# Neighbourhood attention: dividing the softmax on POOL ahead of the transposes

## The chip, the cores and the metric

One core of a Trainium2 chip. The core has five engines, each with its own queue of instructions that it takes in order: TensorE (PE: matrix products and transposes, weight loads shown as PEld), VectorE (DVE), ScalarE (ACT), GpSimd (POOL) and SyncE (SP, which here only issues DMAs). Engines wait for each other by semaphores. The metric is the device time of one execution in microseconds (us), as the median of several; smaller is better.

## What is computed

A two-layer backbone over 2048 latent tokens and 256 context tokens, 1024 wide. The first layer mixes windowed and latent attention; the second, which the change touches, is neighbourhood attention with 16 heads of 64, on a grid of 32 rows by 64 columns:

```python
def row_block(args):                       # one grid row of queries
    ...
    s_loc = einsum('bqhd,bkhd->bhqk', qr, kr) * scale + bias      # 8 x 64 keys around the row
    s_loc = where(mask, s_loc, -inf)                              # 16 columns of them
    s_ctx = einsum('bqhd,blhd->bhql', qr, kc) * scale             # all 256 context keys
    p = softmax(concatenate([s_loc, s_ctx], axis=-1), axis=-1)
    return einsum(p_loc, vr) + einsum(p_ctx, vc)
...
y = (o * silu(z)) @ out_w
h = h + gate * y;  output = rms_norm(h, final_g)
```

The softmax divides each row of exponentials by its sum. It can be divided before the product with V or after it; the change moves this division.

## The kernel before

The program runs its stages one after the other: in0 (input projection of layer 0), attn_a, attn_b, outp(0), in1 (input projection of layer 1), attn_c (the neighbourhood attention) and outp(1) (output projection, residual, last norm). Everything is float32; a product in full precision is made of passes over a rounded part ("h", type fp32r) and a remainder ("l"). Tile's scheduler sets the order of instructions on each engine from its own estimate of times; the code only proposes an order. On the chip that order is fixed.

**attn_c** (from line 1375) has 64 units: 16 heads by 4 column blocks cb of 512 queries. In a unit, `s_pieces` does four row groups rg of 128 queries: four score matmuls into PSUM (`cs`, lines 1475 to 1478, two buffers of two banks), one DVE instruction (line 1482) that adds the bias `cbias` and writes the scores to SBUF (`cp`, 128x640 or 128x768) with their row extremum `cnm`, and one ACT instruction (line 1487) that exponentiates `cp` in place and leaves the row sum in a column of `den`. `t_pieces` and `pv_pieces` (line 647 on) then turn the exponentials around for the product with V: 22 transposes of 128x128 on PE, in six blocks, block j into the PSUM tile `ptc_j` (tag `pt`, three buffers for all of them). Each block is copied out as `phc_j` by ACT (line 239) and as the remainder `plc_j` by DVE (line 240), and PE multiplies V with both into `co` (line 656). ACT copies `co` out as `cos`, and SP stores that to the scratch tensor `s_o`. The transposes of a unit are proposed two units after its scores (`queue`), and the `cp` tiles are two rings of four buffers, two units' worth. POOL makes the bias tiles `cbias` (line 1453) for three of four units.

In the names of instructions, `cp_23` is the tile of column block 2, row group 3, and `ptc_2_0`, `phc_2_0`, `plc_2_0` belong to column block 2, block 0.

Before the change `den` collects the row sums of a head. When the head is done, `den_done` calls `den_piece` (line 672 on): reciprocal on DVE, one transpose on PE (`dnc`, line 677), a copy on DVE and a store to the scratch tensor `s_rd`, 19 times in all.

**outp(1)** goes through four chunks c of 512 tokens. For each it makes G, the gated attention output, in 8 steps j: `load(j)` issues the loads of `o` (two halves), `z` and two row broadcasts of `rd` on SP's queue (lines 1133, 1134, 1136); `comp(j)` adds the halves (line 1147), multiplies by `rd` (line 1148) and by `z` (line 1149), and splits into the high part on ACT (line 1151) and the low one on POOL (line 1152). Lines 1147 and 1148 run on POOL for chunk 0, whose steps lie in attn_c's time, and on DVE for the others. Then 48 matmuls (line 1186) make each of 16 tiles of 128 tokens, with SP loading the residual `rx` (8 DMAs each, line 1172) and storing the result to `out_dram` (line 1221).

Of the kernel before, what the change touches and what calls it, by code (L numbers as in the profile page):

```python
# [8 lines left out]
F32 = mybir.dt.float32  # L9
R32 = mybir.dt.float32r  # L10
BF16 = mybir.dt.bfloat16
AF = mybir.ActivationFunctionType
ALU = mybir.AluOpType
# [3 lines left out]
P = 128  # L17
D = 1024
KB = D // P
TL = 2048  # L20
# [3 lines left out]
NTL = TL // P  # L24
# [76 lines left out]
class Kern:  # L101
    def __init__(self, ctx, tc, ins, out):
        self.tc, self.nc = tc, tc.nc
        self.i, self.out = ins, out
        nc = self.nc
        self.scr = {}

        def scr(name, shape):
            self.scr[name] = nc.dram_tensor("s_" + name, shape, F32, kind="Internal").ap()


        scr("krT", (2, 32, T))
        scr("kaT", (2, 128, T))
        scr("qaT", (2, 512, T))
        scr("qnT", (2, 512, T))
        scr("qrT", (2, 256, T))
        scr("kbT", (2, 512, T))
        scr("qcT", (2, 1024, TL))
        scr("kcT", (2, 1024, T))
        scr("va", (T, 2, 128))  # L120
        scr("vb", (T, 8, 128))

        scr("vc", (16, GRID_W, 4, 8, 128))
        scr("vx", (16, TC, 128))
        scr("z0", (1024, T))
        scr("z1", (1024, TL))
        scr("o0", (2, 1024, T))
        scr("o1", (2, 1024, TL))
        scr("rd0", (16, T))
        scr("rd1", (16, TL))  # L130
        scr("h1", (T, D))
        scr("gate", (2, 2, D))
        scr("one", (1, T))

        cp = self.pool(ctx, "const", 1)
        self.cp = cp
        self.ident = cp.tile([P, P], F32, name="ident")
        make_identity(nc, self.ident)
        self.mhalf = cp.tile([P, 1], F32, name="mhalf")
        nc.gpsimd.memset(self.mhalf, -0.5)  # L140
        one = cp.tile([P, NT], F32, name="one")
        nc.gpsimd.memset(one, 1.0)
        oner = cp.tile([P, NT], R32, name="oner")
        nc.gpsimd.tensor_copy(oner, one)
        self.oner = oner

        self.fac = [cp.tile([P, KB, 2], F32, name=f"fac{l}") for l in range(2)]
        self.sh = [cp.tile([P, KB, 2], F32, name=f"sh{l}") for l in range(2)]
        self.adab = cp.tile([P, 2, 24], F32, name="adab")
        self.ng = cp.tile([P, 2, KB], F32, name="ng")  # L150
# [927 lines left out]
    def outp(self, l):  # L1078
        nc, tc, i, scr = self.nc, self.tc, self.i, self.scr
        with ExitStack() as ctx:  # L1080
# [18 lines left out]
                fg = p.tile([P, D], F32, bufs=1, name="fg")  # L1099
                nc.sync.dma_start(fg, i["fg"].partition_broadcast(P))  # L1100
            chunks = CHUNKS[: 5 - l]
            o_, z_, rd_ = scr[f"o{l}"], scr[f"z{l}"], scr[f"rd{l}"]
            G = {}

            eslots = [(self.E, x) for x in ("vw" if l else "v")]
# [5 lines left out]
            def gsteps(c):  # L1111
                t0, n = chunks[c]
                pl = self.E if c % 2 == 0 else gp
                tags = [("qh", "ql"), ("kh", "kl")] if c % 2 == 0 else [("g0", "g1"), ("g2", "g3")]
                G[c] = [[pl.tile([P, T], R32, tag=t, name=f"G{t}{l}{c}")[:, : 4 * 512].rearrange("p (k t) -> p k t", t=512)
                         if c % 2 == 0 else pl.tile([P, 4, 512], R32, tag=t, name=f"G{t}{l}{c}") for t in tt] for tt in tags]
                ld = {}

                def load(j):
                    if c == 0 or l:  # L1120
                        if c == 0:
                            sl, tag = eslots[j % len(eslots)]
                        else:
                            sl, tag = slots[nld[0] % len(slots)]
                            nld[0] += 1
                        t = sl.tile([P, T if l == 0 else 4 * 512], F32, tag=tag, bufs=1, name=f"o{l}{c}{j}")
                        t = t[:, : 4 * 512].rearrange("p (k t) -> p k t", t=512)
                        o, z, rd = t[:, 0:2], t[:, 2:3], t[:, 3:4]
                    else:
                        o, z, rd = [lp.tile([P, m, 512], F32, tag=x, bufs=b, name=f"{x}{l}{c}{j}")  # L1130
                                    for x, m, b in (("oo", 2, 3), ("oz", 1, 2), ("ord", 1, 2))]
                    js = slice(j * P, (j + 1) * P)
                    nc.sync.dma_start(o[:, :, :n], o_[:, js, t0 : t0 + n].rearrange("e p t -> p e t"))
                    nc.sync.dma_start(z[:, 0, :n], z_[js, t0 : t0 + n])
                    for e in range(2):
                        nc.sync.dma_start(rd[e * 64 : e * 64 + 64, 0, :n],
                                          rd_[2 * j + e : 2 * j + e + 1, t0 : t0 + n].broadcast_to([64, n]))
                    ld[j] = (o, z, rd)

                def comp(j):  # L1140
                    a = ahead[c > 0]
                    if j + a < KB:
                        load(j + a)
                    o, z, rd = ld[j]
                    a = o[:, 0, :n]
                    e1 = nc.gpsimd if c == 0 and l else nc.vector
                    e1.tensor_add(a, a, o[:, 1, :n])
                    e1.tensor_mul(a, a, rd[:, 0, :n])
                    nc.vector.tensor_mul(a, a, z[:, 0, :n])
                    h, lo = [x[:, j % 4, :n] for x in (G[c][0][j // 4], G[c][1][j // 4])]  # L1150
                    nc.scalar.activation(h, a, AF.Copy)
                    nc.gpsimd.tensor_sub(lo, a, f(h))
                return [lambda j=j: load(j) for j in range(ahead[c > 0])] + [lambda j=j: comp(j) for j in range(KB)]


# [219 lines left out]
    def attn_c(self):  # L1375
# [5 lines left out]
        with ExitStack() as ctx:  # L1381
# [9 lines left out]
            pt = self.pool(ctx, "act", 3, psum=True)  # L1391
            op = self.pool(ctx, "aco", 1, psum=True)
            sp = self.pool(ctx, "acs", 2, psum=True)
            DEN = {}

            def den_of(h, cb):

                key, c0 = (h, 0) if h < 15 else ((h, cb), cb * 4)
                if key not in DEN:
                    DEN[key] = r1.tile([P, NTL], F32, tag="den", bufs=3, name=f"denc{h}_{cb}")  # L1400
                return DEN[key], c0

            def den_done(h, cb):
                if h < 15 and cb < 3:
                    return
                d, c0 = den_of(h, cb)
                n = NTL if h < 15 else 4
                self.den_piece(p, pt, d, n, scr["rd1"][h, c0 * P : (c0 + n) * P], f"c{h}_{cb}")

            rm = r1.tile([P, 3, 512], F32, bufs=1, name="rm")  # L1410
            nc.sync.dma_start(rm, i["crm"])

# [44 lines left out]
            def s_pieces(h, cb):  # L1457
# [7 lines left out]
                def go(rg):  # L1465
                    r0, nr = RG[rg]
                    nl = nr * 32
                    qs = slice(cb * 512 + rg * P, cb * 512 + rg * P + P)
                    ps = sp.tile([P, 1024], F32, tag="s", name=f"cs{h}_{cb}{rg}")
                    pl, px, al = ps[:, 512 - nl : 512], ps[:, 512:768], ps[:, 512 - nl : 768]  # L1470
                    bi = b[:, RT[rg], 512 - nl : 768]
                    pl = pl.rearrange("p (t x) -> p t x", x=P)
                    cs = slice(CS[cb] * 4, CS[cb] * 4 + P)
                    rts = slice(r0 // 4, (r0 + nr) // 4)
                    nc.tensor.matmul(pl, q[:, qs], k1v[:, rts, cs], start=True, stop=False)
                    nc.tensor.matmul(pl, q[:, qs], k2v[:, rts, cs], start=False, stop=True)
                    nc.tensor.matmul(px, q[:, qs], k1[:, TL:T], start=True, stop=False)
                    nc.tensor.matmul(px, q[:, qs], k2[:, TL:T], start=False, stop=True)  # L1478
                    n = nl + 256
                    s = pr[n].tile([P, n], F32, name=f"cp{h}_{cb}{rg}")  # L1480
                    nm = r1.tile([P, 1], F32, tag="nm", bufs=16, name=f"cnm{h}_{cb}{rg}")
                    nc.vector.tensor_tensor_reduce(  # L1482
                        out=s[:, :n], in0=al, in1=bi, scale=-1.0, scalar=3.0e38,
                        op0=ALU.add, op1=ALU.min, accum_out=nm)
                    d, c0 = den_of(h, cb)
                    col = cb * 4 + rg - c0
                    self.acts = nc.scalar.activation(s[:, :n], s[:, :n], AF.Exp, bias=nm, scale=-1.0,  # L1487
                                                     accum_out=d[:, col : col + 1]).ins
                    Pt[rg] = s
                return [lambda rg=rg: go(rg) for rg in range(4)], Pt  # L1490

# [40 lines left out]
            def emit_t(sl):  # L1532
                u = queue.pop(0)
                tl = t_pieces(*u)
                old, pend[:] = pend[:], []
                merge(sl, tl)
                den_done(u[0], u[1])
                for s in old:
                    s()

# [144 lines left out]
```

## Time and profile before

| | us |
|---|---|
| median of 3 runs (lowest to highest) | 3622.36 (3619.59 to 3623.66) |
| the profiled execution, its own time | 3611.3 |
| its span, first to last instruction | 3609.5 |
| PE busy, of the span | 3450.7 (96%) |
| DVE busy | 2302.3 (64%) |
| ACT busy | 1904.8 (53%) |
| POOL busy | 1765.0 (49%) |
| attn_c in the trace (first score matmul to the last `ptc`) | 2866 to 3401 |
| outp(1) after it, to the last instruction | 3401 to 3609.5 |

Busy shares are means over stages with different limits, and PE's busy time includes modelled ends of its matmuls. What bounds a stage is read from that stage's windows and its timeline. Times of instructions below come from the one profiled execution, 11 us shorter than the median of the runs.

### The profile page before, as it was taken

The page shows a single profiled execution, that of the slowest core. Times are in us where ns is not written, and L with a number is a line of the kernel's source. Part 1 is how long each engine was busy: PE and PEld are TensorE (multiplying, and loading weights), DVE is VectorE, ACT ScalarE, POOL GpSimd, SP SyncE. Part 2 cuts the span into 40 slices and gives each one's busy share as a digit, 9 for nine tenths or more (in the row PEclk, how much of TensorE's full clock was granted, in tenths as well). Part 3 has the DMA queues.
Part 4 walks back from the last instruction along what each step waited for, and adds up shares of the span by engine and source line. Part 5 has one row for each costly group of instructions (what it writes and reads, how often), then busy time and mean ns, then how long its engine had stood idle before and what let it go on. Part 6 is the DMA issues. An engine that isn't in the chain of part 4 may idle for free.

```text
span 3609.5 us, 52993 instructions
## 1 busy us (share of the span) xinstructions
PE 3450.7 (96%) x17607; PEld 2853.3 (79%) x17607; DVE 2302.3 (64%) x4313; ACT 1904.8 (53%) x3808; POOL 1765.0 (49%) x1655
## 2 busy tenths in 40 slices
PE   6999989999999999999989999999999999999888
PEld 5777779889877777777758778888888899999766
DVE  6445552389999999999978862203110288888565
ACT  4344333389777777777751142223222388888511
POOL 6555544211389999999982262224113133333532
PEclk8999999999999999999999999999999999999999
DMA  6758564673302332213149864544345567666685
GB/s 219 225 196 262 176 188 129 204 204 83 89 16 64 70 69 69 43 38 72 52 140 327 276 193 163 166 112 148 130 129 154 182 250 260 239 228 217 202 236 169
DMA packets 381051, 576.76 MB, mean 160 GB/s; under 512 B 35393, under 2 KB 218081, under 8 KB 370913
## 3 DMA queue, kind: packets, MB, share of 16 engines
q1 hardware_dynamic: 380777, 573.39, 52.2%
q8 instruction: 138, 2.26, 0.3%
q14 instruction: 136, 1.11, 0.1%
HBM read 399.36 MB, written 173.90 MB: 159 GB/s over the span
## 4 chain that ended last, share of the span: by engine, by line
PE 67%; DMA 14%; DVE 6%; issue 5%; POOL 4%; ACT 3%; SPq 1%; DVEq 0%; POOLq 0%; ACTq 0%
PE mm L269 7%; PE mm L268 7%; PE mm L267 7%; PE co L656 4%; DMA adat<-in_adat_dram 4%; PE bo L1000 3%; PE ptc L647 3%; PE bm L943 3%; PE bs L979 3%; PE bs L980 3%; PE bo L1001 3%; PE bs L981 3%; DMA o<-s_o 2%; PE ao L656 2%; PE pta L647 2%
## 5 line engine op out<-in xcount | busy, mean ns | idle before, releaser
L261 POOL TENSOR_TENSOR wl<-ws,wh 128x512 fp32r<-128x512 f32 (+2 forms) x320 | 425.4, 1344 | 638.1 <-ACT wh L260 571.8
L990 POOL TENSOR_TENSOR bacc<-bacc,bph 128x512 f32<-128x512 f32 (+1 forms) x528 | 668.1, 1267 | 35.3 <-ACT bph L984 2.6
L984 ACT ACTIVATE bph<-bs 128x512 fp32r<-128x512 f32 (+1 forms) x610 | 353.4, 579 | 215.0 <-PE bs L981 184.7
L945 DVE TENSOR_REDUCE bmx<-bm 128x1 f32<-128x512 f32 (+1 forms) x656 | 406.4, 628 | 58.8 <-PE bm L943 42.4
L986 DVE TENSOR_TENSOR bpl<-bs,bph 128x512 fp32r<-128x512 f32 (+1 forms) x610 | 401.0, 659 | 16.3 <-ACT bs L985 15.2
L985 ACT ACTIVATE bs<-bs 128x512 f32<-128x512 f32 (+1 forms) x610 | 350.7, 575 | 0.0
L260 ACT ACTIVATE wh<-ws 128x512 fp32r<-128x512 f32 (+2 forms) x328 | 197.5, 613 | 267.1 <-DMA ws<-in_w_dram 215.4
L1453 POOL TENSOR_TENSOR cbias<-cbu,rm 128x384 f32<-128x384 f32 x144 | 158.1, 1110 | 343.7 <-DVE cnm L1482 205.9
L267 PE MATMUL mm<-Uh,wh 128*128 128x512 f32 (+1 forms) x832 | 324.2, 390 | 0.3 <-ACT wh L260 0.3
L268 PE MATMUL mm<-Ul,wh 128*128 128x512 f32 (+1 forms) x832 | 323.7, 389 | 0.0
L269 PE MATMUL mm<-Uh,wl 128*128 128x512 f32 (+1 forms) x832 | 321.8, 390 | 0.4 <-POOL wl L261 0.4
L1482 DVE CUSTOM_DVE_ANT_0 cp<-cs,cbias 128x640 f32<-128x640 f32 (+1 forms) x256 | 222.7, 886 | 134.2 <-PE cs L1478 91.7
L1000 PE MATMUL bo<-bph,bv 128*128 128x512 f32 (+1 forms) x610 | 240.2, 394 | 15.8 <-ACT bos L1005 15.8
L979 PE MATMUL bs<-bqh,bkh 97*128 97x512 f32 (+1 forms) x610 | 242.7, 398 | 12.2 <-DVE bpl L986 11.6
L240 DVE TENSOR_TENSOR plc<-ptc,phc 128x512 fp32r<-128x512 f32 (+1 forms) x384 | 235.3, 640 | 17.5 <-ACT phc L239 16.9
L943 PE MATMUL bm<-bkh,bqh 96*128 96x512 f32 (+1 forms) x656 | 241.9, 384 | 1.9 <-DVE bmx L945 1.6
L1001 PE MATMUL bo<-bpl,bv 128*65 128x512 f32 (+1 forms) x610 | 235.7, 386 | 3.3 <-DVE bos L1007 3.3
L200 DVE SCALAR_TENSOR_TENSOR mj<-adat,scb 128x512 bf16<-128x512 f32 x144 | 120.1, 834 | 185.6 <-DMA adat<-in_adat_dram 168.4
L980 PE MATMUL bs<-bql,bkh 96*128 96x512 f32 (+1 forms) x610 | 238.2, 391 | 0.0
L981 PE MATMUL bs<-bqh,bkl 96*128 96x512 f32 (+1 forms) x610 | 236.6, 388 | 0.0
L1487 ACT ACTIVATE cp<-cp,cnm 128x640 f32<-128x640 f32 (+1 forms) x256 | 226.1, 884 | 16.4 <-DVE cnm L1482 16.1
L239 ACT ACTIVATE phc<-ptc 128x512 fp32r<-128x512 f32 (+1 forms) x384 | 205.7, 560 | 54.6 <-PE ptc L647 48.4
(314 smaller groups left out, 8856.8 us busy)
## 6 DMA issues: line engine op xcount, KB each, us to landing
ws<-in_w_dram SPq DMA_DIRECT2D x256, 256.0 KB
ck<-s_kcT SPq DMA_DIRECT2D x32, 1152.0 KB
cv<-s_vc SPq DMA_DIRECT2D x64, 512.0 KB
adat<-in_adat_dram SPq DMA_DIRECT2D x96, 256.0 KB
o<-s_o SPq DMA_DIRECT2D x40, 512.0 KB
s_z<-zs SPq DMA_DIRECT2D x64, 256.0 KB
s_qcT<-st SPq DMA_DIRECT2D x64, 256.0 KB
s_kcT<-st SPq DMA_DIRECT2D x32, 512.0 KB
```

Of the source, the lines that this page charges most:

```text
L261: (eng or nc.gpsimd).tensor_sub(l[:, :w], s[:, :w], f(h[:, :w]))
L267: nc.tensor.matmul(out, a[0], b[0], start=first, stop=False)
L268: nc.tensor.matmul(out, a[0], b[1], start=False, stop=False)
L269: nc.tensor.matmul(out, a[1], b[0], start=False, stop=last)
L943: nc.tensor.matmul(ps[:, :w], t["qh"][0:96, b * P : (b + 1) * P], t["kh"][0:96, k0 : k0 + w], start=True, stop=True)
L945: nc.vector.tensor_reduce(t["mx"][:, j : j + 1], ps[:, :w], AX.X, ALU.max)
L979: nc.tensor.matmul(ps[:, :n], t["kh"][0:97, ks], t["qh"][0:97, qs], start=True, stop=False)
L984: nc.scalar.activation(hi[:, :n], ps[:, :n], AF.Exp)
L985: self.acts = nc.scalar.activation(ps[:, :n], ps[:, :n], AF.Exp).ins
L986: nc.vector.tensor_sub(lo[:, :n], ps[:, :n], f(hi[:, :n]))
L990: self.pools = nc.gpsimd.tensor_add(st["acc"][:, :n], f((st["h0"] if j == 1 else st["acc"])[:, :n]), f(hi[:, :n])).ins
L1000: nc.tensor.matmul(st["o"][:, :n], t["v"][:, kts[j], 0:P], hi[:, :n], start=fi, stop=la)
```

## The change

Each of the 256 `cp` tiles gets its own 128x1 sum `cd`. After the exponential, DVE takes the reciprocal of that one column, and POOL multiplies the tile by it in place, before the transposes. `den`, `den_piece` and `s_rd` of layer 1 go away; outp(1) loads no `rd` and leaves out the multiplication of line 1148. Layer 0 is as before.

```diff
--- before.py
+++ after.py
@@ in outp
-            o_, z_, rd_ = scr[f"o{l}"], scr[f"z{l}"], scr[f"rd{l}"]
+            o_, z_, rd_ = scr[f"o{l}"], scr[f"z{l}"], scr["rd0"] if l == 0 else None
...
-                    for e in range(2):
+                    for e in range(2 if l == 0 else 0):
                         nc.sync.dma_start(rd[e * 64 : e * 64 + 64, 0, :n],
                                           rd_[2 * j + e : 2 * j + e + 1, t0 : t0 + n].broadcast_to([64, n]))
...
                     e1.tensor_add(a, a, o[:, 1, :n])
-                    e1.tensor_mul(a, a, rd[:, 0, :n])
+                    if l == 0:
+                        e1.tensor_mul(a, a, rd[:, 0, :n])
                     nc.vector.tensor_mul(a, a, z[:, 0, :n])
@@ in attn_c
-            DEN = {}
-            def den_of(h, cb):
...
-            def den_done(h, cb):
...
-                self.den_piece(p, pt, d, n, scr["rd1"][h, c0 * P : (c0 + n) * P], f"c{h}_{cb}")
...
-                    d, c0 = den_of(h, cb)
-                    col = cb * 4 + rg - c0
-                    self.acts = nc.scalar.activation(s[:, :n], s[:, :n], AF.Exp, bias=nm, scale=-1.0,
-                                                     accum_out=d[:, col : col + 1]).ins
+                    d = r1.tile([P, 1], F32, tag="den", bufs=16, name=f"cd{h}_{cb}{rg}")
+                    self.acts = nc.scalar.activation(s[:, :n], s[:, :n], AF.Exp, bias=nm, scale=-1.0, accum_out=d).ins
+
+                    nc.vector.reciprocal(d, d)
+                    nc.gpsimd.tensor_scalar(s[:, :n], s[:, :n], d, None, ALU.mult)
                     Pt[rg] = s
...
                 merge(sl, tl)
-                den_done(u[0], u[1])
```

The scheduler builds another order from this. On PE, in the rows of a unit with column block 2 up to its first products with V (`co_2<-phc_2_0`, `co_2<-plc_2_0`), before:

```order
L647 MATMUL ptc_2_2_32348<-ident,cp_20_32080 128x128
L647 MATMUL ptc_2_2_32348<-ident,cp_23_32173 128x128
L647 MATMUL ptc_2_2_32348<-ident,cp_20_32080 128x128
L647 MATMUL ptc_2_2_32348<-ident,cp_21_32107 128x128
L647 MATMUL ptc_2_3_32359<-ident,cp_20_32080 128x128
L647 MATMUL ptc_2_3_32359<-ident,cp_21_32107 128x128 x2
L647 MATMUL ptc_2_3_32359<-ident,cp_22_32138 128x128
L656 MATMUL co_2_32310<-phc_2_0_32326,cvx_31572 128x512
L656 MATMUL co_2_32310<-plc_2_0_32327,cvx_31572 128x512
L656 MATMUL co_2_32310<-phc_2_1_32335,cvx_31572 128x512
```

and now:

```order
L646 MATMUL ptc_2_0_32657<-ident,cp_22_32454 128x128
L646 MATMUL ptc_2_1_32666<-ident,cp_22_32454 128x128
L646 MATMUL ptc_2_0_32657<-ident,cp_23_32492 128x128
L646 MATMUL ptc_2_1_32666<-ident,cp_23_32492 128x128
L646 MATMUL ptc_2_2_32687<-ident,cp_23_32492 128x128
L646 MATMUL ptc_2_2_32687<-ident,cp_20_32390 128x128
L646 MATMUL ptc_2_2_32687<-ident,cp_21_32420 128x128
L655 MATMUL co_2_32644<-phc_2_0_32662,cvx_31841 128x512
L655 MATMUL co_2_32644<-plc_2_0_32663,cvx_31841 128x512
L646 MATMUL ptc_2_3_32698<-ident,cp_20_32390 128x128
L646 MATMUL ptc_2_3_32698<-ident,cp_21_32420 128x128 x2
L646 MATMUL ptc_2_3_32698<-ident,cp_22_32454 128x128
```

Before, block 0 (`ptc_2_0`) had its four transposes in a row, 16 rows above the first row shown, and the four of block 3 stood ahead of the products too; now the last transpose of block 0 stands five rows ahead of the product with `phc_2_0`, because blocks 0, 1 and 2 are filled together, tile by tile, and block 3 comes behind the product with `plc_2_0`. All 62 units whose transposes run beside later scores end in these rows: `ptc_0`, `ptc_1`, `ptc_2` from row group 3, two more into `ptc_2`, and the products.

On DVE, in the same unit, from its first score instruction (`cp_00`, of a later unit) to the last remainder `plc_2_5`, before:

```order
L1482 ISA cp_00_32316,cnm_00_32317<-cs_00_32311,cbias_28520 128x640
L1482 ISA cnm_00_32317 128x1
L240 TENSOR_TENSOR plc_2_1_32336<-ptc_2_1_32330,phc_2_1_32335 128x512
L240 TENSOR_TENSOR plc_2_2_32354<-ptc_2_2_32348,phc_2_2_32353 128x512
L240 TENSOR_TENSOR plc_2_3_32365<-ptc_2_3_32359,phc_2_3_32364 128x512
L1482 ISA cp_01_32344,cnm_01_32345<-cs_01_32339,cbias_28520 128x768
L1482 ISA cnm_01_32345 128x1
L240 TENSOR_TENSOR plc_2_4_32385<-ptc_2_4_32379,phc_2_4_32384 128x512
L1482 ISA cp_02_32375,cnm_02_32376<-cs_02_32370,cbias_28520 128x768
L1482 ISA cnm_02_32376 128x1
L240 TENSOR_TENSOR plc_2_5_32398<-ptc_2_5_32394,phc_2_5_32397 128x256
```

and now:

```order
L239 TENSOR_TENSOR plc_2_2_32693<-ptc_2_2_32687,phc_2_2_32692 128x512
L1467 ISA cp_00_32650,cnm_00_32651<-cs_00_32645,cbias_28520 128x640
L1467 ISA cnm_00_32651 128x1
L1467 ISA cp_01_32680,cnm_01_32681<-cs_01_32675,cbias_28520 128x768
L1467 ISA cnm_01_32681 128x1
L239 TENSOR_TENSOR plc_2_3_32704<-ptc_2_3_32698,phc_2_3_32703 128x512
L1473 RECIPROCAL cd_00_32653<-cd_00_32653 128x1
L239 TENSOR_TENSOR plc_2_4_32727<-ptc_2_4_32721,phc_2_4_32726 128x512
L1467 ISA cp_02_32714,cnm_02_32715<-cs_02_32709,cbias_28520 128x768
L1467 ISA cnm_02_32715 128x1
L1473 RECIPROCAL cd_01_32683<-cd_01_32683 128x1
L239 TENSOR_TENSOR plc_2_5_32740<-ptc_2_5_32736,phc_2_5_32739 128x256
```

The remainders of blocks 0 to 2 now stand together ahead of the score instructions instead of between them, and the reciprocals stand in DVE's queue behind the exponentials that they read; the other two of the unit follow `cp_03`.

On SP in outp(1), around the last loads of chunk 2 (`o_37092`, `o_37102`, `o_37181`; four DMAs each, as `o_37659` and `o_37666` are the last two after the change with two each), before:

```order
L1134 DMA o_37092<-s_z 128x512
L1136 DMA o_37092<-s_rd 64x512 x2
L1172 DMA rx_36914<-s_h 16x1024 x8
L1221 DMA out_dram<-ry_36972 128x1024
L1133 DMA o_37102<-s_o 128x2x512
L1172 DMA rx_37013<-s_h 16x1024 x8
L1221 DMA out_dram<-ry_37071 128x1024
L1134 DMA o_37102<-s_z 128x512
L1136 DMA o_37102<-s_rd 64x512 x2
L1133 DMA o_37181<-s_o 128x2x512
L1134 DMA o_37181<-s_z 128x512
L1136 DMA o_37181<-s_rd 64x512 x2
```

and now:

```order
L1133 DMA o_37673<-s_o 128x2x512
L1134 DMA o_37673<-s_z 128x512
L1133 DMA o_37749<-s_o 128x2x512
L1134 DMA o_37749<-s_z 128x512
L1173 DMA rx_37165<-s_h 16x1024 x8
L1173 DMA rx_37352<-s_h 16x1024 x2
L1222 DMA out_dram<-ry_37321 128x1024
L1173 DMA rx_37352<-s_h 16x1024 x6
L1222 DMA out_dram<-ry_37361 128x1024
L1133 DMA o_37659<-s_o 128x2x512
L1134 DMA o_37659<-s_z 128x512
L1133 DMA o_37666<-s_o 128x2x512
```

Before, the eighth load of chunk 2 stood behind six stores of output tiles, now behind two.

## Rows read from the trace of the kernel before

**Rows 1.** Windows: stretch, length, busy time of each engine, PEclk, DMA share, GB/s.
```profile
2900.00:3300.00 400.00, 396.41 (x2900) 369.76 (x2900) 347.34 (x724) 347.25 (x753) 133.38 (x120) 1.00 0.69 241
3404.00:3497.00 93.00, 89.09 (x378) 70.01 (x377) 51.75 (x54) 20.37 (x34) 37.65 (x35) 1.00 0.85 239
3497.00:3519.00 22.00, 8.45 (x21) 5.12 (x20) 10.62 (x12) 2.41 (x4) 4.30 (x4) 0.69 0.85 223
```

**Rows 2.** Timeline of PE in attn_c: start, duration, instruction.
```profile
3105.12 0.60 PE L647 MATMUL ptc<-ident,cp 128*128 128x128 f32 x4
3105.47 0.59 PE L656 MATMUL co<-phc,cv 128*128 128x128 f32 x3
```

**Rows 3.** Timeline of ACT in the same stretch; [idle before, releaser].
```profile
3101.02 0.58 ACT L239 ACTIVATE phc<-ptc 128x512 fp32r<-128x512 f32 x1
...
3105.81 0.60 ACT L239 ACTIVATE phc<-ptc 128x512 fp32r<-128x512 f32 x1 [0.65 <-PE ptc L647]
...
3108.34 0.93 ACT L1487 ACTIVATE cp<-cp,cnm 128x768 f32<-128x768 f32 x1
...
3109.26 0.60 ACT L239 ACTIVATE phc<-ptc 128x512 fp32r<-128x512 f32 x1
...
3109.75 0.82 ACT L1487 ACTIVATE cp<-cp,cnm 128x640 f32<-128x640 f32 x1
```

**Rows 4.** Timeline of DVE in the same stretch.
```profile
3101.63 0.69 DVE L240 TENSOR_TENSOR plc<-ptc,phc 128x512 fp32r<-128x512 f32 x1 [0.31 <-ACT phc L239]
...
3106.61 0.69 DVE L240 TENSOR_TENSOR plc<-ptc,phc 128x512 fp32r<-128x512 f32 x1
...
3107.21 0.95 DVE L1482 CUSTOM_DVE_ANT_0 cp<-cs,cbias 128x768 f32<-128x768 f32 x1
...
3108.08 0.42 DVE L240 TENSOR_TENSOR plc<-ptc,phc 128x256 fp32r<-128x256 f32 x1
...
3108.42 0.81 DVE L1482 CUSTOM_DVE_ANT_0 cp<-cs,cbias 128x640 f32<-128x640 f32 x1
...
3109.16 1.43 DVE L240 TENSOR_TENSOR plc<-ptc,phc 128x512 fp32r<-128x512 f32 x2
```

**Rows 5.** Timeline of PE near the end of attn_c, where it waits.
```profile
3374.72 0.50 PE L656 MATMUL co<-plc,cvx 128*128 128x512 f32 x1 [0.92 <-DVE plc L240]
...
3376.25 0.50 PE L1475 MATMUL cs<-ck,cq 128*128 128x512 f32 x1 [0.36 <-DVE cnm L1482]
...
3377.07 0.40 PE L656 MATMUL co<-plc,cvx 128*128 128x512 f32 x1
```

**Rows 6.** Timeline of DVE at the same place.
```profile
3373.98 0.68 DVE L240 TENSOR_TENSOR plc<-ptc,phc 128x512 fp32r<-128x512 f32 x1
...
3374.58 0.17 DVE L675 RECIPROCAL denc<-denc 128x4 f32<-128x4 f32 x1
...
3375.36 0.82 DVE L1482 CUSTOM_DVE_ANT_0 cp<-cs,cbias 128x640 f32<-128x640 f32 x1 [0.61 <-PE ptc L647]
```

**Rows 7.** Groups on POOL by shape: busy us, mean ns, idle before.
```profile
L1453 POOL TENSOR_TENSOR cbias<-cbu,rm 128x384 f32<-128x384 f32 x96 | 97.7, 1019 | 230.5 <-issue 124.3 <-DVE cnm L1482 92.7 <-DMA s_o<-cos 9.4
...
L1453 POOL TENSOR_TENSOR cbias<-cbu,rm 128x512 f32<-128x512 f32 x48 | 62.0, 1292 | 113.2 <-DVE cnm L1482 113.2
...
L765 POOL COPY nmxa<-anm 128x1 f32<-128x1 f32 x144 | 26.7, 186 | 216.9 <-DVE anm L760 216.8
...
L703 POOL COPY amlast<-amask 128x128 f32<-128x128 f32 x1 | 0.3, 291 | 2.4 <-DMA amask<-in_amask_dram 2.4
```

**Rows 8.** Groups by line: the transposes of the sums.
```profile
L677 PE MATMUL dnc<-ident,denc 128*16 128x128 f32 (+1 forms) x19 | 5.1, 271 | 0.0
```

**Rows 9.** Timeline of PE in outp(1).
```profile
3496.80 0.64 PE L1186 MATMUL y<-who,Gkl 128*128 128x512 f32 x2
3508.19 1.22 PE L1186 MATMUL y<-who,Gql 128*128 128x512 f32 x2 [10.75 <-ACT Gql L1151]
```

**Rows 10.** Timeline of SP's queue in outp(1).
```profile
3502.13 2.19 SPq L1136 DMA_DIRECT2D o<-s_rd  x2
```

More of the change, by code (lines that the diff above doesn't have):

```diff
@@ L129, in __init__ @@
         scr("rd0", (16, T))
-        scr("rd1", (16, TL))
         scr("h1", (T, D))
@@ L1393, in attn_c @@
             sp = self.pool(ctx, "acs", 2, psum=True)
-            DEN = {}
-            def den_of(h, cb):
[L1398 to L1401, printed above, removed]
-            def den_done(h, cb):
-                if h < 15 and cb < 3:
-                    return
-                d, c0 = den_of(h, cb)
-                n = NTL if h < 15 else 4
-                self.den_piece(p, pt, d, n, scr["rd1"][h, c0 * P : (c0 + n) * P], f"c{h}_{cb}")
             rm = r1.tile([P, 3, 512], F32, bufs=1, name="rm")
@@ L1484, in go @@
                         op0=ALU.add, op1=ALU.min, accum_out=nm)
-                    d, c0 = den_of(h, cb)
-                    col = cb * 4 + rg - c0
-                    self.acts = nc.scalar.activation(s[:, :n], s[:, :n], AF.Exp, bias=nm, scale=-1.0,
-                                                     accum_out=d[:, col : col + 1]).ins
+                    d = r1.tile([P, 1], F32, tag="den", bufs=16, name=f"cd{h}_{cb}{rg}")
+                    self.acts = nc.scalar.activation(s[:, :n], s[:, :n], AF.Exp, bias=nm, scale=-1.0, accum_out=d).ins
+                    nc.vector.reciprocal(d, d)
+                    nc.gpsimd.tensor_scalar(s[:, :n], s[:, :n], d, None, ALU.mult)
                     Pt[rg] = s
```

## Prediction

> **What bounds the kernel now.** I read the windows of attn_c first, then timelines there to see what follows what, then outp(1), the only other stage that changes. In 400 us of attn_c PE is busy for 396 [rows 1]. A unit gives ACT 15 records (four exponentials, four reads of their sums, six `phc`, one `cos`); 753 records are 50.2 units, so a unit takes 7.97 us. DVE is busy 347 us and ACT 347 us of the 400 (6.9 us per unit each, ends overlapping), POOL 133 us. So here PE sets the pace, DVE and ACT have about a microsecond per unit to spare, and POOL is idle two thirds of the time. In outp(1) PE also sets the pace, except in one hole: it stands for 10.75 us for a high part of G and then runs at a lowered clock [rows 1, 9].
>
> **What a hand-over costs.** The sum below is a chain between engines, so it needs their latencies. Four transposes are issued from 3105.12 and PE is at its next matmul at 3105.47; ACT's copy of that block begins at 3105.81 [rows 2, 3]. So from the moment PE has issued a block's last transpose, `phc` begins 0.34 later, and lasts 0.60. ACT to DVE: the copy of 3101.02 lasts 0.58, the remainder begins at 3101.63 [rows 3, 4], 0.03 later. DVE to PE: a remainder ends at 3374.66, PE goes on at 3374.72; a score instruction ends at 3376.18 and PE's next scores, which need its PSUM buffer, begin at 3376.25 [rows 5, 6]: 0.06 and 0.07. For ACT to PE I take 0.06 as well (estimate from these). Following each other, DVE's instructions take 0.60 (remainder of 512), 0.87 (scores of 768), 0.34 (remainder of 256) and 0.74 (scores of 640) [rows 4]; ACT's take 0.92 (exponential of 768 with its sum), 0.49 (copy) and, by its duration, 0.82 (exponential of 640) [rows 3]. Four score matmuls of the wide kind take PE 0.82 [rows 5].
>
> **What is added to the instruction counts.** Per unit, DVE gets four reciprocals of 128x1. One of 128x4 takes 0.17 [rows 6], and it is never below nothing; I take 0.1 of DVE's time each, 0.4 per unit, which its spare time would hold. POOL gets four multiplications, 704 elements per partition on average, which the trace does not show. From below, a copy, which also reads one tensor: 291 ns for 128 elements, 186 ns for one [rows 7], so 0.83 ns per element and 0.77 us. From above, the two-input add of the bias: 1292 ns for 512, 1019 for 384, so 2.13 ns per element and 1.70 us. The bias itself is 160 us over 64 units, 2.5 us per unit. POOL then needs 5.6 to 9.3 us per unit. I take 0.8 each, since the operation reads one tensor and one number per partition, as the copy does. The Trainium skill (GPSIMD Engine Reference, Engine selection) speaks against this part: elementwise work belongs on VectorE, as two-input operations are about twice as slow on GpSimd, and only one-input ones run roughly at line rate. No run here shows which of the two this is; by the one POOL is near 9.3 us per unit, by the other near 5.6, and the sum below is the same by both.
>
> By these counts alone, nothing would be added to PE's 7.97 us, as a multiplied tile is wanted almost a unit after its exponential.
>
> **What the order adds.** The cost that I expect is in the order. Before, 16 and more rows of PE's queue stood between a block's transposes and its product with V. Now, in each of the 62 units that have both, blocks 0, 1 and 2 are finished at one time and the products stand right behind. Let 0 be the time at which PE has issued the last transpose of block 0. Its four remaining transposes keep it until 0.35. `phc_0` runs 0.34 to 0.94, so the first product begins at 1.00: a wait of 0.65. `plc_0` runs from 0.97 to 1.65, so the second begins at 1.71; the first took about 0.3: a wait of 0.4. Block 3 can't be transposed in that time, as PE's queue is taken in order and it stands behind. After that the copies keep ahead of PE. So PE needs 7.97 + 1.05 = 9.02 us.
>
> There is a second chain, through DVE. PE's last two score groups of a unit need the PSUM buffers of the two before, which DVE frees by its score instructions, and these now stand behind the three remainders. DVE: remainders 0 to 2 from 0.97 to 2.77 and the first scores until 3.51. In 36 of the 62 units (by the order of the changed program) follow remainder 3, scores, reciprocal, remainders 4 and 5 and scores with at most one reciprocal between, last scores: 0.60 + 0.87 + 0.1 + 0.60 + 0.34 + 0.87 + 0.1 + 0.74 = 4.2, to 7.73 (its full end 7.81). PE begins its last scores at 7.88, takes 0.82, and some 0.35 for the last transposes up to block 0's last: 9.05, the same as PE's own 9.02. In 16 units remainder 5 stands ahead of both last scores and waits for its copy on ACT, which stands behind an exponential: copies and exponentials 0.82 + 0.49 + 0.92 + 0.39 from 3.62 on end at 6.24, and 0.03 + 0.34 + 0.87 + 0.74 lead to 8.22, so 9.54. In 10 units a reciprocal that waits for the second exponential stands ahead of them too: 9.65. The mean is (36 x 9.03 + 16 x 9.54 + 10 x 9.65) / 62 = 9.26 us, 1.29 more than now, **80 us** over 62 units.
>
> **What it removes.** In attn_c, 19 transposes of sums on PE [rows 8], at about 0.09 of its time each (four take 0.35 [rows 2]), 2 us; the first transposes wait for reciprocal and multiplication once, about 2 us the other way. These cancel. In outp(1), 64 loads of `rd`, of which 48 (chunks 1 to 3) lie on its path, go from SP's queue, and 24 multiplications from DVE. Their place is the hole [rows 1, 9]: between 3497 and 3519 PE did 10 pairs of matmuls, 4.6 us of work, in 22 us, so 17 us are lost. The last pair of `rd` loads of chunk 2 was issued at 3502 to 3504 [rows 10], behind the stores of six tiles. Now chunk 2's last load stands behind two stores, some 40 us of PE's work earlier, so I expect the hole to close: between nothing and 20 us (a smaller hole at chunk 3 with it); I take **15 us**.
>
> Sum: 80 - 15 = +65 us. On the profiled execution's own 3611.3 that is 3676; the runs' median is 11 us above it, so I forecast 3687 us.
>
> **The rivals.**
> 1. PE has room that the busy time hides. In the same window the weight loads are busy 370 of 400 us [rows 1]. By the Trainium skill (Perfetto Trace Analysis, Identifying the Most-Contended Engine) matmul busy time says little on the distance from the limit and the weight loads' share does: 8% would be free, 0.6 us per unit. Whatever the reading, if 0.6 us of a unit is slack, the 9.02 becomes 8.4, the second chain is what is left, and a cost of about 45 us remains: 3652. Against it speaks the timeline, where rows follow each other without a gap.
> 2. The order costs nothing, since copies and products overlap in some way that I miss: attn_c stays at 7.97 and the closed hole shows, with 2 us for the sums: 3605, faster. It decides for "faster" below 0.15 us added per unit. Against it: PE is seen to stand 0.92 us for a remainder with transposes right behind it in its queue [rows 5].
> 3. POOL becomes the bound. At the price of a two-input add it needs 9.3 us per unit, no more than the chain; it must reach 1.9 us per multiplication to give 10.1 us, 130 us in all: 3737. In favour: the trace has no such instruction. Against: the copy's price.
> 4. The hole stays, because the stores of other tiles hold the `z` loads: 3702, inside the first case's range.
>
> **How the numbers follow.** The forecast case has a chance of 0.65 (with rival 4 in it), rival 1 of 0.13, rival 3 of 0.08; rival 2 has 0.10 as faster and 0.04 as a loss that the hole pays back to within 0.2% (7 us, about what a measurement of this kernel can tell from no change). The forecast's own range is 9.0 to 9.65 us for all units and 0 to 20 us for the hole: 3666 to 3726. With rival 1 and part of rival 3 it is 3645 to 3735.
>
> **What would show it.** PE waiting in each unit for `phc` about 0.65 us and for `plc` about 0.4 us; units of 9.0 to 9.7 us, so attn_c some 80 us longer; waits of score matmuls for `cnm`; multiplications on POOL of 0.7 to 1.0 us with POOL idle for a third or more; reciprocals of about 0.1 to 0.15 us that wait for exponentials; in outp(1) no wait near 10 us ahead of chunk 2. It would be wrong if PE waits for POOL's result ahead of its transposes, or if PE shows no waits for `phc` and `plc`.

## The result, and the profile after

The changed kernel takes 3765.4 us (median of 6 runs), 1.0411 times the kernel before (95% interval 1.04 to 1.0421). The forecast was 3687 us with a range of 3645 to 3735: the sign was right, the size wrong by 78 us. The profiled span is 3763.8 us, 154 longer than before. Of these, 6 lie ahead of attn_c; from its first score matmul to its last transpose it now takes 696 us (2872.3 to 3568.0), 161 more; from there to PE's last matmul 185 us, 13 less.

The windows that answer to [rows 1]: attn_c, then outp(1).
```profile
2900.00:3300.00 400.00, 345.18 (x2175) 296.91 (x2174) 272.68 (x677) 271.28 (x567) 400.00 (x241) 0.94 0.52 185
...
3565.00:3580.00 15.00, 9.73 (x46) 7.84 (x46) 9.23 (x12) 4.54 (x9) 6.63 (x5) 0.77 0.94 314
3580.00:3610.00 30.00, 29.84 (x130) 23.77 (x128) 16.14 (x12) 9.47 (x16) 23.30 (x16) 1.00 0.85 281
3610.00:3620.00 10.00, 4.99 (x18) 3.44 (x17) 9.90 (x9) 1.89 (x3) 6.71 (x5) 0.77 0.81 233
3620.00:3750.00 130.00, 130.00 (x559) 105.66 (x558) 80.44 (x71) 25.89 (x44) 38.26 (x44) 0.99 0.61 187
```
POOL, the last busy time, stands at 400.00 of 400: it never rests, where before it worked 133 us. PE fell from 396 to 345, DVE and ACT from 347 to about 272. ACT's 567 records at 15 per unit are 37.8 units, so a unit takes 10.58 us against 7.97. In outp(1) the stop of 10.75 us [rows 9] is gone; two smaller ones (15 us and 10 us long, PE two thirds and half busy) are left.

The groups on POOL by shape, which answer to [rows 7]:
```profile
L1474 POOL TENSOR_SCALAR cp<-cp,cd 128x768 f32<-128x768 f32 x128 | 297.7, 2371 | 0.0
L1474 POOL TENSOR_SCALAR cp<-cp,cd 128x640 f32<-128x640 f32 x128 | 259.4, 2050 | 0.6 <-DVE cd L1473 0.6
```
A multiplication takes 2.37 or 2.05 us from its start to its end, and POOL stands 0.6 us in all ahead of 256 of them: the next one is always there already. POOL's instructions overlap a little, so what one costs is read from start to start:
```profile
3198.62 2.06 POOL L1474 TENSOR_SCALAR cp<-cp,cd 128x640 f32<-128x640 f32 x1
3200.47 1.45 POOL L1438 TENSOR_TENSOR cbias<-cbu,rm 128x512 f32<-128x512 f32 x1
3201.72 2.39 POOL L1474 TENSOR_SCALAR cp<-cp,cd 128x768 f32<-128x768 f32 x1
3203.89 1.20 POOL L1438 TENSOR_TENSOR cbias<-cbu,rm 128x384 f32<-128x384 f32 x1
```
The multiplication of 640 holds POOL for 1.85 us and that of 768 for 2.17; the means of those that another instruction follows at once are 1.86 and 2.18. Two of each are 8.1 us per unit, and the bias by the same reading 2.4, so 10.5 us, against 10.58 measured.

What PE waits for in 600 us of attn_c (total, times, longest), and examples of the first two in PE's timeline, with POOL's at that place:
```profile
PE ptc L646 <- POOL cp L1474: 51.9, 50, 1.7
PE co L655 <- ACT phc L238: 19.2, 50, 1.4
PE co L655 <- DVE plc L239: 11.3, 50, 0.2
```
```profile
3218.63 0.44 PE L646 MATMUL ptc<-ident,cp 128*128 128x128 f32 x2 [0.43 <-POOL cp L1474]
3220.49 0.76 PE L646 MATMUL ptc<-ident,cp 128*128 128x128 f32 x5 [1.42 <-POOL cp L1474]
3221.56 0.51 PE L655 MATMUL co<-phc,cvx 128*128 128x512 f32 x1 [0.31 <-ACT phc L238]
```
```profile
3213.98 6.45 POOL L1474 TENSOR_SCALAR cp<-cp,cd 128x768 f32<-128x768 f32 x3
```
Three multiplications back to back end at 3220.43, and PE's transposes start at 3220.49. The waits for `phc` and `plc` that the forecast spoke of are there too, but those for POOL set the pace. PE waiting for POOL's result ahead of its transposes is a sign that the forecast had named for being wrong.

### The profile page after: what moved, and what is told of

It reads as the page before. It is cut to its first block, busy times and chain, and to the rows that moved or that the text cites. A ratio compares the mean times of both kernels' runs of the same rounds, so it can differ in the third digit from the quotient of the medians.

```text
span 3763.8 us, 53708 instructions
## 1 busy us (share of the span) xinstructions
PE 3531.0 (94%) x17588; PEld 2888.8 (77%) x17588; DVE 2316.3 (62%) x4507; ACT 1918.3 (51%) x3808; POOL 2273.3 (60%) x1903
## 4 chain that ended last, share of the span: by engine, by line
PE 65%; DMA 9%; POOL 8%; issue 7%; DVE 6%; ACT 3%; SPq 1%; POOLq 0%; ACTq 0%; DVEq 0%
PE mm L268 7%; PE mm L267 7%; PE mm L266 7%; PE y L1187 5%; POOL cp L1474 4%; PE bo L999 3%; PE bm L942 3%; PE bs L978 3%; PE bo L1000 3%; PE bs L979 3%; PE bs L980 3%; PE co L655 3%; DMA adat<-in_adat_dram 2%; PE ptc L646 2%; PE ao L655 2%
## 5 line engine op out<-in xcount | busy, mean ns | idle before, releaser
L1474 POOL TENSOR_SCALAR cp<-cp,cd 128x640 f32<-128x640 f32 (+1 forms) x256 | 540.1, 2210 | 0.6 <-DVE cd L1473 0.6
L646 PE MATMUL ptc<-ident,cp 128*128 128x128 f32 x1408 | 261.3, 293 | 58.3 <-POOL cp L1474 58.2
L646 PEld LDWEIGHTS ptc<-ident,cp 128*128 128x128 f32 x1408 | 183.8, 150 | 89.5 <-POOL cp L1474 71.4
```

Source lines behind the costliest of these rows:

```text
L646: nc.tensor.transpose(ps[:, col : col + P], src(), ident)
L1474: nc.gpsimd.tensor_scalar(s[:, :n], s[:, :n], d, None, ALU.mult)
```

## The experiments

Two theories were tried. **P**: POOL sets the pace, by the price of its multiplication. **O**: the order of PE's queue sets it, as forecast. Whether the order has the price that the forecast gave it is a question of its own: the dearer of the two demands hides the other. A ratio is to the kernel before, run on the same chip, with its 95% interval. The us per unit come from ACT's records in the window from 2900 to 3300, as above.

**The form of the multiplication.** The line that the change adds on POOL, in four versions:
```
 nc.gpsimd.tensor_scalar(s[:, :n], s[:, :n], d, None, ALU.mult)                     # changed kernel
 nc.gpsimd.tensor_tensor(s[:, :n], s[:, :n], d.broadcast_to([P, n]), ALU.mult)      # a_two_input
 nc.vector.tensor_scalar(s[:, :n], s[:, :n], d, None, ALU.mult)                     # b_on_dve
 nc.gpsimd.tensor_scalar(s[:, :n], s[:, :n], 0.5, None, ALU.mult)                   # i_constant_factor
```


> The multiplication stays on POOL but is written as one of two tensors, the second the reciprocal repeated along the row. Theory P (POOL sets the pace of attn_c, at 2.0 to 2.2 us per multiplication with one number per partition): the price changes to that of the bias add, 2.13 ns per element, so 1.5 us for 704 elements and up to 1.7 with its start; 4 x 1.6 + 2.3 = 8.7 us per unit against 10.6, so 1.3 to 1.9 us less per unit, 3650 to 3690 us in all, with POOL still nearly full. If this form costs as much as the other, 3765 again and POOL full. Theory O (the order of PE's queue costs the time, as I forecast): the price of the multiplication doesn't matter, the time moves only with the order, 3740 to 3790.

Measured: 1.0011 (1.0001 to 1.0021), faster than either theory allowed. POOL's groups:
```profile
L1474 POOL TENSOR_TENSOR cp<-cp,cd 128x768 f32<-128x768 f32 x128 | 189.0, 1487 | 1.9 <-DVE cd L1473 1.5
L1474 POOL TENSOR_TENSOR cp<-cp,cd 128x640 f32<-128x640 f32 x128 | 160.4, 1260 | 19.0 <-PE ptc L646 9.2 <-DVE cd L1473 8.5 <-PE cs L1463 1.2
```
With two tensors to read it takes 1.49 and 1.26 us (1.43 and 1.21 from start to start), a third less than with one tensor and one number per partition. The expectation took the bias add's 2.13 ns per element and 1.6 us each; this form is cheaper than that too, 1.77 ns by the two durations. A unit takes 8.22 us. The scheduler also laid PE's rows in another order, so this run alone does not part price and order.

> The multiplication is done by DVE. POOL then has only the bias, 2.5 us per unit. Theory P: POOL is out, and DVE is next: 6.9 us per unit of before, 0.64 for four reciprocals of 0.16, and four multiplications; at the pace of the score instructions (0.74 and 0.87) 3.2 us, so 10.7 us per unit and some 3770; at half of that, 9.1 and some 3670. Theory O: the units cost what their waits for phc and plc add, whoever multiplies, and a busier DVE adds to it: above 3765.

Measured: 1.0204 (1.0185 to 1.0223). DVE is the full engine, the third busy time:
```profile
2900.00:3300.00 400.00, 377.74 (x2479) 326.05 (x2478) 398.37 (x945) 312.43 (x649) 126.22 (x104) 0.99 0.60 211
```
A unit takes 9.24 us, against 9.1 worked out from DVE's needs at the faster price; its multiplications take 0.67 us on average.

> The same POOL instruction in shape and place, its factor the constant 0.5 in place of the reciprocal's address (the output is not divided). It asks what makes the multiplication dear. If reading one number per partition does, the price falls to the copy's 0.83 ns per element, some 0.8 us, POOL to 5.5 us per unit and the time to 3600 to 3650. If it is the form, the price stays at 1.9 to 2.4 us, POOL stays full and the time at 3745 to 3770.

Measured: 1.0342 (1.0327 to 1.0358), 10.29 us per unit, POOL full.
```profile
L1474 POOL TENSOR_SCALAR cp<-cp 128x768 f32<-128x768 f32 x128 | 274.6, 2153 | 0.0
L1474 POOL TENSOR_SCALAR cp<-cp 128x640 f32<-128x640 f32 x128 | 233.5, 1831 | 0.4 <-ACT cp L1471 0.4
```
From start to start these take 2.10 and 1.78 us, 0.08 less than with a number per partition (2.18 and 1.86), and the unit is 0.29 us shorter, 0.07 for each of four. So reading the number from an address is worth 0.08 us; the form itself is dear. At 3739 us the run lies 6 us below the range that was expected. Nor does the price of the changed kernel's form move with what stands around it: it is 1.85 to 1.86 and 2.18 to 2.20 us in `d_half_multiplied`, `g_code_order` and `p_before_order` below too. Why this form is dear no run shows.

**Less of it.** `c_no_division` drops the reciprocal and the multiplication, `d_half_multiplied` keeps the multiplication for blocks 0 and 2 (`if rg % 2 == 0:` ahead of it).

> Neither reciprocal nor multiplication in attn_c (its part of the output is not divided by the sums), no loads of reciprocals in the output projection. It parts the change's gain from its price. Theory P (POOL's multiplication is the whole loss): attn_c falls back to the 535 us of before and the output projection keeps its 183 us from the last transpose to the last matmul, against 199 before: 3595 to 3605. Theory O (blocks that follow their exponentials directly are filled together and cost waits): attn_c stays some tens of us longer, above 3625.

> POOL multiplies, with one number per partition as in the changed kernel, only blocks 0 and 2 of each unit's four (one of 640, one of 768; the others are not divided). POOL needs 2 x 2.0 + 2.3 = 6.3 us per unit and is no bound. In two of three units the order of PE's queue still has blocks 0 to 2 filled together ahead of the products. Theory P: attn_c within 20 us of before, 3600 to 3625 in all, POOL busy some 75 to 80%. Theory O, by the forecast's own 1.29 us for such a unit: 2/3 x 62 x 1.29 = 53 us of waits, 3645 to 3660.

Measured: 0.998 (0.997 to 0.9989) and 0.9987 (0.9976 to 0.9998). Attn_c takes 545 and 541 us, 8.12 and 8.15 per unit, and 181 and 185 us follow it. With half the multiplications POOL is no bound:
```profile
2900.00:3300.00 400.00, 389.95 (x2822) 361.13 (x2821) 351.46 (x879) 340.81 (x736) 327.11 (x217) 1.00 0.68 238
```
The second run lies within P's numbers, the first 4 us above them, and both are far from O's. But here too the scheduler chose another order, so O's price of the changed kernel's own order was not yet tried.

**The order alone.** `g_code_order` takes PE's rows in attn_c in the order of the code; `m_same_order` and its kin write the 2944 transposes, products and score groups of attn_c out one by one, as the changed kernel has them; `p_before_order` and its kin as the kernel before has them:
```
+ ctx.enter_context(tc.manual_schedule(engines={mybir.EngineType.PE}))
...
+ for ch in SEQ:          # one letter for each transpose, product or score group
+     t = TOKS[ch]
...
```


> As the changed kernel, but PE's queue in attn_c has the order in which the code is written (a score group or two between each two blocks), not the scheduler's. Blocks 0 to 2 are no longer filled together ahead of the products. Theory P: POOL still sets the pace at 10.3 to 10.6 us per unit, so 3745 to 3800, POOL full in attn_c. Theory O: with the order gone, the cost goes with it: 3610 to 3690.

> The same order of PE's queue, with the multiplication left out (the output is not divided by the sums). Theory P: without POOL's work the time falls by 60 to 150 us below the run with the same order and the multiplication; with the code's order itself at 8.0 to 9.3 us per unit, 3600 to 3690. Theory O: within 15 us of the run with the same order and the multiplication.

> A control: the rows of PE's queue in attn_c are written out in the order that the changed kernel has, row for row, instead of being found by the scheduler; the work is the changed kernel's. Both theories: as the changed kernel, 3750 to 3780, POOL full in attn_c. What differs from 3765 is due to the order of the other engines.

> The control without the multiplication (the output is not divided): PE's rows in attn_c in exactly the changed kernel's order, so all 62 units have blocks 0 to 2 filled together right ahead of the products, but POOL has only the bias. It measures the term that the forecast put at 1.29 us per unit. Theory O (as forecast): units of 9.0 to 9.65 us, attn_c 615 us and 183 behind it, 3665 to 3690. Theory P (POOL is the whole loss): waits of 0.5 for phc and 0.2 for plc in a unit at most, the rest caught up: units of 8.0 to 8.7 us, 3600 to 3645.

> The changed kernel's work with PE's rows of attn_c in exactly the order of the kernel before (without its transposes of sums). Theory P: POOL's price alone is enough, whatever the order: 10.4 to 10.6 us per unit, POOL full, 3740 to 3765. Theory O, or a price that adds to the order's: without the order's 57 us the time is 3690 to 3715.

> The changed kernel's order of PE in attn_c, row for row, and the multiplication of two tensors on POOL, 7.9 us per unit. Only the price differs from the changed kernel. If time is the larger of the order's 9.0 us per unit and POOL's: 9.0, 3665 to 3685, as the run without the multiplication. If the two add: 3720 or more.

Measured, ratio with interval, and us per unit (the scheduler's row has another order in each column; without multiplication its kernel, `c_no_division`, leaves out the reciprocal too, the two above it keep it):

| PE's order | one number per partition, POOL | two inputs, POOL | no multiplication |
|---|---|---|---|
| changed kernel's, written out | 1.0404 (1.039 to 1.0418), 10.58 | 1.0142 (1.0129 to 1.0156), 9.02 | 1.0151 (1.0138 to 1.0165), 9.02 |
| kernel before's, written out | 1.0437 (1.0421 to 1.0454), 10.66 | 1.0028 (1.0017 to 1.0038), 8.28 | not run |
| the code's | 1.0414 (1.0396 to 1.0431), 10.60 | not run | 1.0273 (1.0252 to 1.0293), 9.72 |
| the scheduler's own | 1.0411 (1.04 to 1.0421), 10.58 | 1.0011 (1.0001 to 1.0021), 8.22 | 0.998 (0.997 to 0.9989), 8.12 |

The control gives the changed kernel's time again. Down the first column the time hardly cares for the order: POOL is at 400 of 400 in each, here with the order of before (3770 us, 5 above P's range),
```profile
2900.00:3300.00 400.00, 325.20 (x2148) 290.07 (x2148) 276.92 (x672) 273.39 (x563) 400.00 (x241) 0.94 0.52 186
```
and PE waits for POOL (PE ptc) in place of `phc`:
```profile
PE ptc L1561 <- POOL cp L1506: 93.5, 64, 3.7
```
Along the first row the order has its price as soon as POOL is cheap: 9.02 us per unit, the same with a POOL that is 349 us busy (two inputs) and one that is 119 us busy (none). So the larger of the two demands decides, and they do not add. In this row O's numbers for the order are met (3672 us, and 3664, 1 below its range). The code's order has a price of its own, 9.72 us per unit, so `g_code_order_undivided` takes 3710 us, 20 above P's number, and in that order the multiplication costs 50 us, not 60 or more. The windows of `m_same_order_two_input` and `m_same_order_undivided`, and PE's timeline in the latter:
```profile
2900.00:3300.00 400.00, 369.64 (x2544) 326.12 (x2544) 313.58 (x793) 313.53 (x665) 349.47 (x283) 1.00 0.60 213
2900.00:3300.00 400.00, 369.56 (x2543) 325.91 (x2542) 313.48 (x791) 313.56 (x665) 119.05 (x107) 1.00 0.60 212
```
```profile
3212.71 0.71 PE L1560 MATMUL ptc<-ident,cp 128*128 128x128 f32 x5
3213.73 0.50 PE L1571 MATMUL co<-phc,cvx 128*128 128x512 f32 x1 [0.31 <-ACT phc L269]
3214.45 0.50 PE L1571 MATMUL co<-plc,cvx 128*128 128x512 f32 x1 [0.23 <-DVE plc L270]
```
The five transposes are issued in 0.44 us (0.088 each [rows 2]), until 3213.15, and the product starts 0.58 later; the next one 0.72 later, of which its predecessor explains 0.3. These 0.58 and 0.42 us stand where the forecast had waits of 0.65 and 0.4.

**Versions that might beat the kernel before.** `k_eighth_on_dve` and `l_eighth_on_act` take the two-input form on POOL, but give the last block of every second unit to DVE or ACT (`if rg == 3 and cb % 2:`); `p_before_order_two_input` is in the table, and `p_before_order_act` is it with ACT's eighth.

> The multiplication of two tensors on POOL, but for one block in eight (the last of every second unit, 640 elements), which DVE multiplies in 0.67 us. POOL goes from 7.9 to 7.3 us per unit, DVE from 7.2 to 7.5. Theory P: PE becomes the bound again at 8.0 us per unit, 535 to 545 us of attn_c and 183 behind it: 3595 to 3608, faster than before. If the 8.2 us of the run with two inputs came from waits for phc and plc and not from POOL, nothing changes: 3610 to 3622.

> The multiplication of two tensors on POOL, but for one block in eight (the last of every second unit, 640 elements), which ACT multiplies, some 0.7 us. ACT goes from 7.0 to 7.4 us per unit, POOL from 7.9 to 7.3. Theory P with every engine below PE's 8 us: 3598 to 3612, the 10 us that POOL's load still costs are won. If ACT's multiplication delays the copies that PE waits for: 3615 to 3640.

> The order of the kernel before and the multiplication of two tensors on POOL, 7.9 us of POOL per unit. With the price and the order both mended, attn_c is 535 to 550 us and the output projection keeps its 16 us: 3590 to 3612, faster than before. If POOL, as full as PE, delays the transposes in this order: 3615 to 3640.

> As the run with the order of before and two inputs, but ACT multiplies one block in eight (640 elements). POOL has 7.3 us per unit, ACT 7.4. If POOL's load is what is left: 3590 to 3605 and below the run with two inputs alone; if not, the same as that run within 6 us.

Measured: 1.0026 (1.0014 to 1.0038), 0.9986 (0.9974 to 0.9999), 1.0028 (1.0017 to 1.0038) and 1.0024 (1.0015 to 1.0033). Three are 0.24 to 0.28% slower than the kernel before; ACT's eighth is at most 0.26% faster, its median 0.5 us above the range that was expected of it at best. From the first score to the last transpose these kernels need 554 to 562 us against 535 before, which eats the gain of outp(1). In the order of before PE still waits for the two-input form on POOL, 14.7 us in 13 places, in the stretch from 2860 to 3440. Why attn_c needs 545 us even with no division is not settled; the order of before without the multiplication was not run.

**The loads of outp(1).** Two edits to the kernel before, attention untouched: one load for the two of a block, or the two issued from ACT's queue.
```
- for e in range(2): nc.sync.dma_start(rd[e * 64 : e * 64 + 64, 0, :n], rd_[2 * j + e : ...].broadcast_to([64, n]))
+ nc.sync.dma_start(rd[:, 0, :n], rd_[2 * j : 2 * j + 2, ...].unsqueeze(1).broadcast_to([2, 64, n]))   # n_one_load
+ for e in range(2): nc.scalar.dma_start(rd[e * 64 : e * 64 + 64, 0, :n], ...)                         # q_loads_apart
```


> The kernel before with one edit: in the output projection the two loads of reciprocals of a block are one, so that 32 fewer transfers go through SP's queue; attention is untouched. If the number of transfers in that queue makes the hole ahead of chunk 2 (10.75 us), it shrinks or closes and the time is 3595 to 3608; if the loads wait for data or buffers, nothing changes: 3609 to 3617.

> The kernel before with one edit: in the second output projection the loads of reciprocals are issued from ACT's queue instead of SP's; attention is untouched and nothing is left out. It asks whether the forecast's reason for the hole ahead of chunk 2 holds (the loads stand in SP's queue behind stores). If so, the hole of 10.75 us and its lowered clock go, 12 to 18 us: 3594 to 3602, faster than both kernels. If the loads wait for something else, or ACT's copies now wait for their issue: 3608 to 3625.

Measured: 1.0257 (1.0243 to 1.0271), much slower, and 1.0023 (1.0014 to 1.0032). With one load attn_c takes 565 us, 30 more than before, and what follows it 67 more; with the loads apart attn_c takes 545, and what follows it 199 as before. What DVE waits for, first with one load, then with the loads apart:
```profile
DVE o L1151 <- DMA o<-s_rd: 81.6, 17, 8.6
```
```profile
DVE o L1147 <- DMA o<-s_o: 30.3, 12, 5.9
DVE o L1149 <- DMA o<-s_z: 22.6, 3, 19.6
```
With the reciprocals in another queue PE's stop stays (13.3 us for `Gql` in three pieces). It now hangs on the loads of `o` and `z`, which still stand right behind a store in SP's queue; SP, DVE and PE:
```profile
3503.13 0.37 SPq L1221 DMA_DIRECT2D out_dram<-ry  x1
3503.59 0.38 SPq L1133 DMA_DIRECT2D o<-s_o  x1
```
```profile
3510.09 0.69 DVE L1147 TENSOR_TENSOR o<-o 128x512 f32<-128x512 f32 x1 [3.73 <-DMA o<-s_o]
```
```profile
3513.76 1.03 PE L1186 MATMUL y<-who,Gql 128*128 128x512 f32 x2 [4.68 <-ACT Gql L1151]
```
So to move the reciprocals' loads alone does not close the stop. That the place of loads behind stores made it is neither shown nor refuted. The kernels without these loads need 12 to 18 us less after attn_c, but they also leave out a multiplication and some traffic; which of these helped stays open. Nor does `n_one_load` answer it, since its one load lands later than the pair (last section).

## Why the prediction was wrong

- **The step that failed** is the price of POOL's multiplication: "I take 0.8 each", between bounds of 0.77 and 1.70. It measured 2.18 and 1.86 us from start to start in the changed kernel (2.37 and 2.05 long), 2.0 on average, above the upper bound. Four of them and the bias are 10.5 us per unit (10.58 measured), more than the 9.0 of the order. The bound was taken from the two-input add as the dearest form in the trace; the form used stood there only on tiles of 1 to 8 elements per partition, and at this size it was dearer than that. The 0.8 itself leaned on one copy of 128 elements. The other half of the remark, that the sum is the same by either price, held for 0.8 and 1.7 alone. That the sign came out right is luck as far as the mechanism goes: POOL's 10.58 us hide the order's 9.02, which the forecast had in mind.
- **Rival 3** (chance 0.08) is what happened, at 10.6 us in place of 10.1, past its own threshold of 1.9 us per multiplication.
- **The order's 80 us** were nearly right as a demand of PE, and the `m_same` runs show it: 9.02 us per unit as forecast for PE's chain, and attn_c 73 us longer than before (608 against 535) without the multiplication and 64 with the two-input form. The second chain, through DVE, which took the mean to 9.26, did not come: `cs` waits for `cnm` 1.8 us in all in the two-input run. Had POOL's price been as forecast, the time would have been about that of these runs, 3664 to 3672 us.
- **Rival 1**, that 0.6 us of a unit is slack because the weight loads' share is 92%, is refuted by the same 9.02: all of PE's waits showed up in the unit. The Trainium skill (Perfetto Trace Analysis, Identifying the Most-Contended Engine) names the weight loads' share, beside the FLOPs achieved, as a measure of the distance from the limit. Here a share of 92% did not mean that the other 8% could take up waits: 1.05 us of them made the unit 1.05 us longer.
- **Rival 2**, that the order costs nothing, is wrong for the changed kernel's order, but with cheaper forms the scheduler found orders with units of 8.12 to 8.22 us, 0.15 to 0.25 longer than before; what these are owed to is not settled.
- **outp(1)**: 15 us were forecast and 13 measured here, 12 to 18 in the other kernels that leave these loads out. The size held; the reason given, the loads' place behind stores, is neither shown nor refuted.
- **Reciprocals**: 0.1 us forecast, 0.16 measured, hidden in DVE's spare time as said.

## What to carry to other kernels

Before work goes to an idle engine, multiply the price of its exact form by the count per unit and compare the sum with the pace of the stage; where the trace lacks that form, the dearest other form is no upper bound, and a rival at twice the price needs a real chance. Demands on different engines in one stage don't add: the largest decides, and mending it lays the next one bare, here the order of PE's rows. A scheduler lays rows anew when an operation changes, so to part a price from an order, write the order out and vary the price alone.

## What the runs showed of the hardware

On POOL, multiplying 128x768 takes 2.18 us from start to start with one number per partition, 2.10 with a constant, and 1.43 with a second tensor that repeats the number. The Trainium skill (GPSIMD Engine Reference, Engine selection) has two-input work about twice as slow as on VectorE and one-input work roughly at line rate. The first agrees in size (an add of 128x512 takes 1.29 us on POOL and 0.69 on DVE); the second does not for this form, where the measurement decides.

DVE's multiplication is slow where it starts beside a POOL instruction. In `b_on_dve`, DVE and then POOL:
```profile
3102.26 1.52 DVE L1474 TENSOR_SCALAR cp<-cp,cd 128x640 f32<-128x640 f32 x1
...
3105.77 0.60 DVE L1474 TENSOR_SCALAR cp<-cp,cd 128x768 f32<-128x768 f32 x1
```
```profile
3102.15 1.28 POOL L1438 TENSOR_TENSOR cbias<-cbu,rm 128x512 f32<-128x512 f32 x1 [2.87 <-DVE cnm L1467]
3104.61 1.02 POOL L1438 TENSOR_TENSOR cbias<-cbu,rm 128x384 f32<-128x384 f32 x1 [1.17 <-DVE cd L1473]
```
The 640 elements that start while POOL adds take 1.52 us and end 0.35 after the add; the 768 that meet no add take 0.60. Of the run's 256 multiplications, the 94 that start during a POOL instruction all end 0.35 to 0.42 us after it and take 0.88 on average (up to 1.64); the other 162 take 0.57, none over 0.62. It goes the other way too: POOL's adds of 128x384 that start during a DVE multiplication take 1.27 us, the others 1.04. The Trainium skill (SBUF — State Buffer, SBUF: two separate sides) says that such instructions of the two engines hold a shared port for their whole length and block each other; the trace agrees. In `k_eighth_on_dve`, with POOL nearly full, the mean is 1.21 us, which may be why DVE's eighth brought nothing; no run parts it from the rest.

One load that repeats two rows over 128 partitions lands late. In `n_one_load`, SP's queue and the DVE instruction that reads this load:
```profile
3432.99 0.54 SPq L1136 DMA_DIRECT2D o<-s_rd  x1
```
```profile
3447.63 0.69 DVE L1151 TENSOR_TENSOR o<-o 128x512 f32<-128x512 f32 x1 [5.78 <-DMA o<-s_rd]
```
Its reader starts 14.1 us after the issue is done. Of a pair of loads of one row each, in the kernel before, it starts 7.2 us after, again SP's queue and DVE:
```profile
3433.14 1.09 SPq L1136 DMA_DIRECT2D o<-s_rd  x2
```
```profile
3441.43 0.69 DVE L1148 TENSOR_TENSOR o<-o 128x512 f32<-128x512 f32 x1 [1.28 <-DMA o<-s_rd]
```
Over the 24 readers on DVE the median is 14.3 us with one load (7.8 to 16.8) and 5.9 with the pair (3.3 to 9.3). Why it lands late no run shows.
